# The attention loop of a two-layer encoder, with all its matmuls in 64 rows of the array

## The chip, the cores and the metric

The kernel runs as one program on one core of a Trainium2 chip. The metric is the device time of one execution in microseconds (us). The core has a matrix engine (PE) with its weight load (PEld), three engines for elementwise work (DVE, ACT, POOL), a queue that issues DMAs (SP; POOL and ACT issue some too), an on-chip memory of 128 partitions (SBUF), and an accumulator memory (PSUM) of eight banks of 128 x 512 fp32, into which PE writes and from which DVE and ACT read.

## The reference, cut to what matters

Two layers over two sequences (2048 and 512 tokens, width 1024), each with an RMS norm, a mixer, a SiLU gate, an output projection and a residual. Only the attention layer is touched by the change:

```python
def attention_layer(x, g, w_in, w_out, sink, rel_bias):
    h = rmsnorm(x, g)
    z = h @ w_in                  # q: 16 heads of 64, k and v: 4 heads of 64, gate: 1024
    ...
    # 128-query blocks, each against three 128-key blocks
    scores = einsum('bnqhgd,bnkhd->bnhgqk', qb, kw) * scale + bias
    p = exp(scores - m); denom = p.sum() + exp(sink - m)
    o = einsum('bnhgqk,bnkhd->bnqhgd', p / denom, vw)
    return x + (o * silu(gate)) @ w_out
```

Products are made to near-fp32 precision from two parts of each operand: every logical product of two tiles is three matmuls, high by high, high by low and low by high.

## The kernel before, in words

**Chunks.** The 2560 tokens go through the attention layer in five chunks of 512: chunk 0 is the short sequence, chunks 1 to 4 the long one. Each chunk makes its normalised input (`make_h`), projects k and v (`kv_proj`, L353), and then runs the attention loop (L909) over n = 0 to 16. The output projection of a chunk (`out_proj`, L653) begins inside the loop and ends after it. The Fourier layer follows all chunks.

**One turn of the loop.** A turn works on two query blocks of a head pair p: scores, softmax, transposes, product with v. It is software-pipelined by one turn: in turn n the scores are made of "new" blocks (head pair n // 2, blocks 0, 1 or 2, 3), while the "old" blocks of turn n - 1 are transposed and multiplied by v. Between these, PE works off "fill": the q and gate projections of later head pairs, eight units a turn (a unit is a product of one contraction block k with its three matmuls of 128 x 512; L966 and L980), and near the end the output projection.

**Steps, with their lines.** `scores` (L524; matmuls L530) multiplies q by the key window; the contraction is 64 long, so the two heads of a pair stand in the two halves of the array's rows and run as pairs of 64-row matmuls. `biased` (L545, DVE L549) adds the bias and finds the row maximum, `exps` (ACT L557) takes the exponential, `divide` (DVE reciprocal L565, DVE L569 or ACT L567) normalises. `transp` (L575; PE L589) transposes 64 x 64 pieces, in 64 rows too. `parts` (ACT L597, DVE L598) copies them out of PSUM as a high and a low part. `av` (L600; PE L615) multiplies by v with all 128 rows. `out_evac` copies half of the result to SBUF (ACT L624, tile `t`), adds the other half to it (DVE L633, twice), and POOL, ACT and POOL apply the gate and split the result into tile `uT` (L635, L638, L639). A finished projection is evacuated by `evac_q` (ACT L465, DVE L466) or `evac_g` (ACT L473, DVE L475); in chunk 0 the helper `scaled` first scales it by the norm (DVE L350).

**PSUM.** Each bank is a tile of its own: four turn over in the pool `psum` through `bank` (L76) for projections, transposes, `av` and the output projection, and four (`spt`, L332) hold the scores, one of them also a transpose.

**What sets the order.** `seq` and `pe` (L164, L170) chain the instructions of PE, ACT and DVE inside the loop, each behind the one before it, so each engine runs them in the order in which the code is written. Waits between engines are put in when the program is built: an instruction waits until the counter of another engine has reached the value that the last conflicting access to the same tile sets. In this program they are kept by tile.

## Time and profile before

| | us |
|---|---|
| runs, median of 3 (lowest to highest) | 1570.89 (1569.17 to 1573.85) |
| profiled execution: span from first to last instruction | 1566.4 |
| what lies around the span, median less span | 4.5 |

The page gives no other time of the profiled execution than its span. In the trace the loops of the chunks begin (first matmul of the first q projection) at 30.5, 241.8, 451.1, 664.2 and 871.4 us of the span, and the last `av` of each ends at 184.1, 399.0, 612.1, 825.2 and 1027.5 us; the Fourier layer takes the last third. The page's first part is busy time by engine, the second the span in 40 slices, the fourth the chain of work that ended last, followed back from the last instruction. A row of that chain gives the start of a piece and how long the chain ran in it, so for back-to-back matmuls it gives the time that they took one after the other, whereas a row of the timeline gives the time from the first start to the last end, in which overlapping instructions are merged.

### The profile page before, as it was taken

The page shows a single profiled execution, that of the slowest core. Times are in us where ns is not written, and L with a number is a line of the kernel's source. Part 1 is how long each engine was busy: PE and PEld are TensorE (multiplying, and loading weights), DVE is VectorE, ACT ScalarE, POOL GpSimd, SP SyncE. Part 2 cuts the span into 40 slices and gives each one's busy share as a digit, 9 for nine tenths or more (in the row PEclk, how much of TensorE's full clock was granted, in tenths as well). Part 3 has the DMA queues.
Part 4 walks back from the last instruction along what each step waited for, and adds up shares of the span by engine and source line. Part 5 has one row for each costly group of instructions (what it writes and reads, how often), then busy time and mean ns, then how long its engine had stood idle before and what let it go on. Part 6 is the DMA issues. An engine that isn't in the chain of part 4 may idle for free.

```text
span 1566.4 us, 27701 instructions
## 1 busy us (share of the span) xinstructions
PE 1555.5 (99%) x9818; PEld 1306.6 (83%) x9818; DVE 1178.3 (75%) x2843; ACT 877.1 (56%) x2120; POOL 446.7 (29%) x614
## 2 busy tenths in 40 slices
PE   9999999999999999999999999999999999999998
PEld 7888888888898888988888888888888888888886
DVE  5888555887548886378873588767999888989886
ACT  7788534676237774256761476636556564333353
POOL 2575642421403413124224142123121211101100
PEclk9999999999999999999999999999999999999999
DMA  8588696665865576756749665675675569656852
GB/s 295 203 330 297 222 369 208 214 242 202 294 228 196 207 267 231 245 190 234 267 150 322 239 235 196 227 258 203 217 249 189 195 243 399 210 202 250 296 193 95
DMA packets 100423, 372.34 MB, mean 238 GB/s; under 512 B 11204, under 2 KB 22220, under 8 KB 82877
## 3 DMA queue, kind: packets, MB, share of 16 engines
q1 hardware_dynamic: 82716, 297.38, 54.2%
q0 software_dynamic: 16400, 70.04, 11.5%
q10 hardware_dynamic: 1168, 3.15, 0.6%
q8 instruction: 78, 1.28, 0.3%
q14 instruction: 61, 0.49, 0.1%
HBM read 280.06 MB, written 90.47 MB: 237 GB/s over the span
## 4 chain that ended last, share of the span: by engine, by line
PE 92%; DVE 3%; issue 2%; DMA 1%; POOL 0%; ACT 0%; SPq 0%; POOLq 0%; DVEq 0%; ACTq 0%
PE gp L117 15%; PE qp L117 14%; PE spt L117 11%; PE op L117 7%; PE av L615 6%; PE spt L530 6%; PE W L117 5%; PE fo L117 5%; PE vp L117 3%; PE Wo L117 3%; PE Z L117 3%; PE pt L589 3%; PE Zo L117 2%; PE z L1166 2%; PE ABp L117 1%
## 5 line engine op out<-in xcount | busy, mean ns | idle before, releaser
L117 PE MATMUL gp<-h,wg 128*128 128x512 f32 x960 | 237.8, 396 | 0.0
L117 PE MATMUL qp<-h,wq 128*128 128x512 f32 x960 | 237.1, 396 | 0.0
L549 DVE CUSTOM_DVE_ANT_0 S<-spt,b 128x385 f32<-128x385 f32 (+1 forms) x320 | 161.0, 529 | 98.9 <-PE spt L530 62.4
L117 PEld LDWEIGHTS gp<-h,wg 128*128 128x128 f32 x960 | 174.9, 188 | 37.3 <-issue 1.0
L117 PEld LDWEIGHTS qp<-h,wq 128*128 128x128 f32 x960 | 174.9, 188 | 36.5 <-issue 0.3
L557 ACT ACTIVATE S<-S 128x385 f32<-128x385 f32 (+1 forms) x320 | 190.7, 610 | 15.7 <-DVE S L549 15.7
L597 ACT CAST pts<-pt 128x384 fp32r<-128x384 f32 (+1 forms) x240 | 95.1, 462 | 179.3 <-PE pt L589 176.5
L598 DVE TENSOR_TENSOR pts<-pt,pts 128x384 fp32r<-128x384 f32 (+1 forms) x240 | 112.5, 519 | 22.4 <-ACT pts L597 22.2
L639 POOL TENSOR_TENSOR uT<-o,uT 128x256 fp32r<-128x256 f32 x75 | 55.5, 740 | 234.2 <-ACT uT L638 234.1
L117 PE MATMUL spt<-wo,uT 128*128 128x512 f32 x480 | 120.3, 391 | 0.0
L117 PE MATMUL op<-wo,uT 128*128 128x512 f32 x480 | 118.9, 391 | 0.0
L615 PEld LDWEIGHTS av<-pts,v 128*128 128x128 f32 x576 | 101.4, 188 | 18.8
L615 PE MATMUL av<-pts,v 128*128 128x512 f32 (+1 forms) x576 | 115.7, 341 | 0.0
L117 PE MATMUL fo<-wo,tTu 128*128 128x512 f32 x480 | 115.0, 392 | 0.0
L569 DVE TENSOR_SCALAR S<-S 128x384 f32<-128x384 f32 (+1 forms) x192 | 103.2, 537 | 6.8
L117 PEld LDWEIGHTS op<-wo,uT 128*128 128x128 f32 x480 | 89.4, 188 | 18.5
L117 PEld LDWEIGHTS spt<-wo,uT 128*128 128x128 f32 x480 | 89.1, 188 | 18.3
L530 PE MATMUL spt<-kwin,qab 64*128 64x384 f32 (+1 forms) x960 | 104.1, 343 | 0.0
L117 PEld LDWEIGHTS fo<-wo,tTu 128*128 128x128 f32 x480 | 88.3, 188 | 17.3
L530 PEld LDWEIGHTS spt<-kwin,qab 64*128 64x128 f32 x960 | 75.5, 184 | 28.2 <-issue 25.0
L635 POOL TENSOR_TENSOR o<-o,s 128x256 f32<-128x256 f32 x75 | 55.1, 735 | 129.4 <-DVE o L633 128.6
L589 PEld LDWEIGHTS pt<-ident,S 64*128 64x128 f32 x1328 | 69.8, 138 | 4.4 <-issue 1.8
(342 smaller groups left out, 3207.3 us busy)
## 6 DMA issues: line engine op xcount, KB each, us to landing
wo<-wsd SPq DMA_DIRECT2D x32, 1024.0 KB, 6.5
wq<-wsd SPq DMA_DIRECT2D x31, 1024.0 KB, 7.7
wg<-wsd SPq DMA_DIRECT2D x31, 1024.0 KB, 6.3
x<-x1d SPq DMA_DIRECT2D x40, 512.0 KB, 3.5
b<-b21d SPq DMA_DIRECT2D x40, 512.0 KB, 4.6
b<-rowd SPq DMA_DIRECT2D x40, 384.0 KB, 4.4
xs<-in_x_dram SPq DMA_DIRECT2D x23, 512.0 KB, 6.6
s2d<-gt POOLq DMA_DIRECT2D x40, 256.0 KB, 4.3
```

The lines of the kernel that those rows point to most:

```text
L117: ins = pe(PE.matmul(out, a[i], b[j], start=start and i + j == 0, stop=stop and i == 1, skip_group_check=more))
L530: pe(PE.matmul(banks[j][:, 2 + k0 * P : 2 + k1 * P], res["q"][rows, qp, b * P : (b + 1) * P], kwin[g][rows, kp, b * P + k0 * P : b * P + k ...
L549: seq(DVE, DVE.tensor_tensor_reduce(out=s[:, e0:e1], in0=ps[:, 1 + e0 : 1 + e1], in1=st["bias"][:, j, 386 - e1 : 386 - e0][:, ::-1], scale ...
L557: last_exp[0] = seq(ACT, ACT.activation(s[:, e0:e1], s[:, e0:e1], AF.Exp, bias=s[:, 386:387], scale=-1.0, accum_out=s[:, 387:388]))
L569: seq(DVE, DVE.tensor_scalar(s[:, ks], s[:, ks], den, None, ALU.mult))
L589: pe(PE.transpose(ps[h][:, kb, j, :], ss[j][rows, 1 + kb * P : 1 + (kb + 1) * P], ident[rows, rows]))
L597: seq(ACT, ACT.copy(hi, ps[:, k0:k1]))
L598: seq(DVE, DVE.tensor_tensor(lo, ps[:, k0:k1], f32(hi), ALU.subtract))
L615: pe(PE.matmul(to, v, pt, start=n == part == 0, stop=part == 1 and n in (1, len(todo) - 1), skip_group_check=n > 1,))
L635: eng.tensor_tensor(o, o, s, ALU.mult)
L639: low = eng.tensor_tensor(lo, o, f32(hi), ALU.subtract)
L1166: PE.matmul(to, m[part][:, g * P : (g + 1) * P], ch[:, 0, :, odd * P : (odd + 1) * P], start=part == 0, stop=part == 1,)
```

## The change

All matmuls of the loop now use 64 rows. A product of 128 rows is split into its upper and lower 64 rows; an upper half of one product runs beside a lower half of another, each into its own bank (`beside`). Since the halves of one product meet in one bank, a PE `nop` waits for the last matmul of the one half before the other half begins there (`swapped`). Projections and output tiles go through a new class `Product`, in the order `fills(n)` lists: in turn n the first twelve pairs finish the lower rows of projection n + 1 beside the first upper rows of projection n + 2, the second twelve finish the upper rows of n + 2 beside the first lower rows of n + 3. `av` is split by query block: block 0 in the upper rows beside block 1 in the lower, then the other way round, with three pairs of fill between them. A block's product takes six matmuls of 256 columns in each half, where before two blocks shared matmuls of 512 columns.

The eight banks are now two tiles of four banks each, `pj` (projections and `av`) and `spt` (banks 0, 1 scores, banks 2, 3 transposes), so there are two banks of scores and two of transposes where there were four and three. The turn is written in another order: transpose of the first old block, scores of the first new block, twelve pairs of fill, transpose of the second, scores of the second, nine pairs, first half of `av`, three pairs, second half. `out_evac` of a turn is moved into the next turn, ahead of the copies of `parts`; the evacuation of a projection stands between the softmax of the first and the copies of the second block. Weights are loaded one projection at a time, a little over two turns ahead. The norm's transposes (`spread_halves`) use 64 rows. In `kv_proj` the products go to `spt` and `pj`; the Fourier layer's pool `psum2` is opened after the old pools are closed.

```diff
-    banks = [pstack.enter_context(tc.tile_pool(name="psum", bufs=4, space=PSUM))]
+    banks = []
+    pj = pstack.enter_context(tc.tile_pool(name="psum", bufs=1, space=PSUM)).tile([P, 4, 512], F32, name="pj")
+    spt = pstack.enter_context(tc.tile_pool(name="spsum", bufs=1, space=PSUM)).tile([P, 4, 512], F32, name="spt")
...
+            def beside(*pairs):
+
+                swapped([(unit[0].last, h) for pair in pairs for h, unit in enumerate(pair) if unit is not None])
+                for upper, lower in pairs:
+                    both = []
+                    for h, unit in enumerate((upper, lower)):
+                        if unit is not None:
+                            both.append((unit[0], h) + unit[0].parts(unit[1], slice(64 * h, 64 * h + 64)))
+                    for i, j in ((0, 0), (0, 1), (1, 0)):
+                        for out, h, a, b in both:
+                            out.last[h] = pe(PE.matmul(out.ps, a[i], b[j], **out.flags()))
+
+            def swapped(places):
...
+                if before:
+                    wait = pe(PE.nop())
+                    for ins in before:
+                        tc.add_manual_dep(wait.ins, ins.ins.name, DONE, reason="other rows of a bank")
...
-                    ps = [bank(f"pt{c}_{p}_{b}_{h}")[:, :384] for h in range(2 - second)]
-                    if second:
-                        ps.append(spt[0][:, 2:386])
-                    ps = st["pt", b] = [t.rearrange("p (k j q) -> p k j q", k=3, j=2) for t in ps]
+                    ps = [spt[:, 2 + h, :384].rearrange("p (k j q) -> p k j q", k=3, j=2) for h in range(2)]
...
+                def fills(n):
+
+                    t0, t1, t2, t3 = op_tiles
+                    if n < 14:
+                        x, y, z = (o + (t3,))[n + 1 : n + 4]
+                        return [((y, k), (x, 4 + k)) for k in four], [((y, 4 + k), (z, k)) for k in four]
...
                     if new:
                         one, two = order
                         on_act = new[1] if c else one
-                        new[0].scores(one, spt[:2])
...
+                        new[0].scores(one)
+                    split = out_evac() if out_evac else None
+                    if old:
+                        old[0].parts(older[0])
...
+                    beside(*first)
...
+                    if n < 15:
+                        evacs[n + 1]()
+                        loads[n + 5]()
                     if old:
                         old[0].transp(older[1], 1)
...
+                    cut = 2 if n == 14 else 3
+                    beside(*second[:cut])
                     if old:
...
+                        if n > 14:
+                            places = Both(spt[:, 0:2])
+                        elif n % 4 == 3:
+                            places = [pj[:, 3], pj[:, 0]]
+                        else:
+                            places = Both(pj[:, n % 4 : n % 4 + 2])
+                        halves = old[0].av(old[1], places)
+                        halves[0]()
+                    beside(*second[cut : cut + 1])
```

How the order moves is shown for turn 5 of chunk 2, where the old blocks are blocks 0 and 1 of head pair 2 and projection 6 (q of pair 3) is finished. First PE before, from the last transpose (out to `spt`) over the second half of q's fill (`qp`) to `av` and the gate's fill (`gp`):

```order
L589 MATMUL spt_233<-ident,S_2_1_1_6090 128x64
L117 MATMUL qp_3_6141<-h_4_5121,wq_3_5905 128x512 x3
L117 MATMUL qp_3_6141<-h_5_5130,wq_3_5905 128x512 x3
L117 MATMUL qp_3_6141<-h_6_5138,wq_3_5905 128x512 x3
L117 MATMUL qp_3_6141<-h_7_5146,wq_3_5905 128x512 x3
L615 MATMUL av_2_0_6243<-pts_2_0_6174,v_4_3036 128x512 [waits DVE_49,Activation_49]
L615 MATMUL av_2_0_6243<-pts_2_0_6174,v_4_3036 128x512 [waits DVE_49]
L615 MATMUL av_2_0_6243<-pts_2_0_6174,v_5_5500 128x512 x2
L615 MATMUL av_2_0_6243<-pts_2_0_6174,v_3_3008 128x256 x2
L615 MATMUL av_2_0_6243<-pts_2_0_6174,v_6_5503 128x256 x2
L117 MATMUL gp_3_6269<-h_0_5088,wg_3_5907 128x512 [waits DMAHW5_49,PE_49]
```

The fill between the transposes and `av` waits for no other engine; `av` waits for the transposed parts. PE in the changed kernel, from the end of the `av` before, over the first transpose and the first scores to the first fill:

```order
L658 MATMUL pj<-pts_1_2_7378,v_7_6703 128x256
L623 MATMUL spt<-ident,S_2_0_0_7410 128x64 [waits DVE_49]
L623 MATMUL spt<-ident,S_2_0_0_7410 128x64 x5
L623 MATMUL spt<-ident,S_2_0_1_7412 128x64 x6
L570 MATMUL spt<-kwin,qab_2_7282 128x384 x6
L480 MATMUL pj<-h_0_6274,wg_3_7129 128x512 [waits DVE_49,PE_49,Activation_49]
L480 MATMUL pj<-h_4_6307,wq_3_6963 128x512
L480 MATMUL pj<-h_0_6274,wg_3_7129 128x512
```

The first fill now waits for DVE, ACT and PE: the value of DVE's counter is the one that the second add of `out_evac` (L684 in the changed kernel, on the `av` just ended) sets, ACT's is that of its copy (L675), and PE's is the `nop`'s. The fill writes banks 2 and 3 of `pj` here, the adds read banks 0 and 1. Further on in the same turn, from the end of the first fill to the second:

```order
L480 MATMUL pj<-h_7_6332,wq_3_6963 128x512
L623 MATMUL spt<-ident,S_2_1_0_7475 128x64 [waits DVE_49]
L623 MATMUL spt<-ident,S_2_1_0_7475 128x64 x5
L623 MATMUL spt<-ident,S_2_1_1_7477 128x64 x6
L570 MATMUL spt<-kwin,qab_2_7282 128x384 x6
L480 MATMUL pj<-h_4_6307,wg_3_7129 128x512 [waits DVE_49]
L480 MATMUL pj<-h_0_6274,wq_4_7285 128x512 [waits DMAHW6_49]
L480 MATMUL pj<-h_4_6307,wg_3_7129 128x512
```

The second fill waits for the value that DVE's last instruction of `evac_q` (L516) sets on the projection that the first fill has just finished; it writes banks 3 and 0, the evacuation reads bank 2. The transpose waits for the second `biased` of the new block, which reads banks 0 and 1 of `spt`, where the transpose writes banks 2 and 3. Last, ACT in the changed kernel, from the copy of `out_evac` to the copies of the second old block, with q's evacuation as the eighth row:

```order
L675 COPY t_1_2_7561<-pj 64x512 [waits PE_49]
L632 CAST pts_2_0_7542<-spt 128x6x64 [waits PE_49,Activation_49]
L632 CAST pts_2_0_7542<-spt 128x6x64 [waits DVE_49]
L594 ACTIVATE S_2_2_0_7571<-S_2_2_0_7571 128x385 [waits DVE_49]
L594 ACTIVATE S_2_2_1_7573<-S_2_2_1_7573 128x385 [waits DVE_49]
L689 CAST uT_1_6786<-o_1_2_7563 128x256 [waits Pool_49]
L604 ACTIVATE S_2_2_1_7573<-S_2_2_1_7573 128x384 [waits DVE_49]
L515 ACTIVATE qab_3_7608<-pj 128x512 [waits PE_49]
L632 CAST pts_2_0_7542<-spt 128x6x64 [waits PE_49]
L632 CAST pts_2_0_7542<-spt 128x6x64 [waits DVE_49]
```

Before, q's evacuation stood behind all four copies and all four exponentials of a turn and ahead of `out_evac`; now it stands behind the first block's exponentials and ahead of the second block's copies, and `out_evac` opens the turn.

## The prediction

> **What bounds the kernel now.** I read the page's first two parts, then the chain of waits by engine and line, then the chain in order of time over single turns.

> ```profile
> span 1566.4 us, 27701 instructions
> PE 1555.5 (99%) x9818; PEld 1306.6 (83%) x9818; DVE 1178.3 (75%) x2843; ACT 877.1 (56%) x2120; POOL 446.7 (29%) x614
> PEclk9999999999999999999999999999999999999999
> PE 92%; DVE 3%; issue 2%; DMA 1%; POOL 0%; ACT 0%; SPq 0%; POOLq 0%; DVEq 0%; ACTq 0%
> ```

> PE is busy throughout, at the full granted clock, and 92% of the chain is PE's. So before, DVE (75%) and ACT (56%) have room, and their work costs nothing as long as it lands under matmuls. One turn of chunk 3 in the chain (start, duration):

> ```profile
> 743.21 1.25 PE spt L530 x12
> 744.46 0.43 PE pt L589 x13
> ...
> 745.26 2.95 PE gp L117 x12
> 748.21 1.38 PE av L615 x8
> 749.59 2.75 PE qp L117 x12
> 752.34 0.71 PE spt L530 x5
> ```

> The turn takes 752.34 - 743.21 = 9.13 us and holds no wait: scores 1.25, transposes 0.80 (between 744.46 and 745.26, the rows in between are more of the same), gate fill 2.95, `av` 1.38, q fill 2.75. Twelve matmuls cost 2.75, 0.229 each; 2.95 stands after the 64-row transposes, so going into 128 rows costs 0.20.

> **The change part by part.** *Switches.* A turn goes into 128 rows once (0.20) and back once; scores that open the turn take 1.25, those that follow other 64-row work 1.14 (chunk 1's row below has 1.08), so the way back is 0.11. All in 64 rows saves 0.31 a turn, 75 turns: 23 us. That is the gain.

> *The pairs.* A pair of 64-row matmuls of 512 columns is not in this trace. From below: scores in pairs of 384 columns take 1.14/6 = 0.19; the columns that a 128-row fill streams would take 0.229 x 384/512 = 0.172, so at worst the overhead of 0.018 stays and a pair of 512 is about 0.241 (the line through the 64-column transposes, 0.063 a pair, and 0.19); at best 0.203 (part of the 0.229 being the exposed load). I take 0.229, as the streamed columns are the same, and keep -0.026 x 24 x 75 = -47 and +0.012 x 24 x 75 = +22 for the range. The row of loads that bears on it:

> ```profile
> L117 PEld LDWEIGHTS gp<-h,wg 128*128 128x128 f32 x960 | 174.9, 188 | 37.3 <-issue 1.0
> L530 PEld LDWEIGHTS spt<-kwin,qab 64*128 64x128 f32 x960 | 75.5, 184 | 28.2 <-issue 25.0
> ```

> A 128-row load of 0.188 passes beside matmuls spaced 0.229. [...]

> *New waits.* This is the large term. The order of PE shows that in the changed program the first fill of a turn waits for DVE's second add and ACT's copy of the `av` just ended, and the second fill waits for DVE's evacuation of the projection that the first fill finishes. Neither reads the bank that is written; `pj` is one tile and conflicts are kept by tile. Also the transposes wait for both `biased` of a block that reads the other banks of `spt`. Before, each bank was a tile and these waits were not there. So PE stands, and all of its queue behind it: the weight loads, transposes, scores, hence ACT and DVE too. The durations, from chunk 3:

> ```profile
> 744.87 1.25 ACT L597 CAST pts<-pt 128x384 fp32r<-128x384 f32 x3 [3.02 <-PE pt L589]
> 745.98 0.51 ACT L597 CAST pts<-spt 128x384 fp32r<-128x384 f32 x1
> 746.36 0.65 ACT L557 ACTIVATE S<-S 128x385 f32<-128x385 f32 x1
> 746.87 0.22 ACT L557 ACTIVATION_READ_ACCUMULATOR S<-S 128x1 f32 x1
> 746.97 0.64 ACT L557 ACTIVATE S<-S 128x385 f32<-128x385 f32 x1
> 747.57 0.42 ACT L638 CAST uT<-o 128x256 fp32r<-128x256 f32 x1
> 747.86 0.64 ACT L557 ACTIVATE S<-S 128x385 f32<-128x385 f32 x1
> ...
> 749.12 0.62 ACT L567 ACTIVATE S<-S 128x384 f32<-128x384 f32 x1
> 749.65 0.58 ACT L473 ACTIVATE th<-gp 128x512 f32<-128x512 f32 x1
> 750.25 0.58 ACT L624 COPY t<-av 64x512 f32<-64x512 f32 x1
> ```
> ```profile
> 745.17 0.56 DVE L549 CUSTOM_DVE_ANT_0 S<-spt,b 128x385 f32<-128x385 f32 x1
> 745.65 1.48 DVE L598 TENSOR_TENSOR pts<-pt,pts 128x384 fp32r<-128x384 f32 x3
> ...
> 748.18 0.84 DVE L569 TENSOR_SCALAR S<-S 128x384 f32<-128x384 f32 x1
> 748.94 0.21 DVE L565 RECIPROCAL S<-S 128x1 f32<-128x1 f32 x2
> 749.18 0.42 DVE L569 TENSOR_SCALAR S<-S 128x384 f32<-128x384 f32 x1
> ...
> 750.33 0.69 DVE L475 SCALAR_TENSOR_TENSOR s<-th,gp 128x512 f32<-128x512 f32 x1 [0.19 <-ACT th L473]
> ```
> ```profile
> L633 DVE TENSOR_TENSOR o<-av,t 64x256 f32<-64x256 f32 x150 | 62.5, 416 | 8.2 <-ACT t L624 5.7 <-ACT b L510 1.5
> 665.18 0.26 ACT L370 CAST kwin<-spt 64x128 fp32r<-64x128 f32 x1 [0.54 <-DVE kwin L371]
> 665.48 0.28 DVE L371 TENSOR_TENSOR kwin<-spt,kwin 64x128 fp32r<-64x128 f32 x1 [0.33 <-ACT kwin L370]
> ```

> The last two rows give the hand-over between engines: 665.18 + 0.26 to 665.48, 0.04. Now a turn of the changed kernel by hand, with 0 at the end of the last `av` matmul:

> - PE: transposes of one block 0.80/2 = 0.40, scores 0.57 (half of 1.14), done at 0.97.
> - ACT's copy 0.04 to 0.62; DVE's adds from 0.72 (0.10, as between th's end at 750.23 and 750.33) and 1.15, done at 1.57. With a hand-over and 0.20 to get PE going again (estimate: the price of the switch, 0 to 0.4) the first fill starts at 1.81, not 0.97. **First stall 0.84.** It ends at 1.81 + 2.75 = 4.56.
> - ACT: copies of the transposes 1.01 and 1.38; DVE: their low parts 1.58 and 2.04, `biased` 2.51 and 2.99 (done 3.07, 3.55); ACT: exponentials 3.11 and 3.72 with the accumulator's read to 4.45, `uT` within. DVE: reciprocal and normalising 3.88 to 4.49, second reciprocal by 4.65; ACT's normalising 4.69 to 5.21.
> - Evacuation: behind that in ACT's order, 5.22 to 5.80; DVE's part 5.84 to 6.53. Transposes and scores of the second block pass under it (4.56 to 5.53). Second fill at 6.53 + 0.04 + 0.20 = 6.77, not 5.53. **Second stall 1.24.** Without the evacuation waiting behind the softmax it could start 0.6 earlier; ACT's order forbids it.
> - Nine pairs 2.06, half of `av` 0.69, three pairs 0.69, half of `av` 0.69: end at 10.90. The low parts of the second block are done near 7.5, so `av` waits for nothing.

> So a turn takes 10.90 against 9.13: +1.77, which is 0.84 + 1.24 less 0.31. (PE alone: 8.82.) The other chunks' turns:

> ```profile
> 897.39 2.99 PE gp L117 x12
> ...
> 904.26 1.08 PE spt L530 x12
> ...
> 915.11 2.95 PE gp L117 x12
> ```
> ```profile
> 142.70 2.97 PE gp L117 x12
> ...
> 151.30 2.94 PE qp L117 x12
> ```

> Chunks 1 and 4 take (915.11 - 897.39)/2 = 8.86 a turn, chunk 0 takes 151.30 - 142.70 = 8.60. They have the same chain on ACT and DVE and shorter scores, so after 10.77 and, with chunk 0's extra scaling in each evacuation on DVE, 11.0. Sum: 30 x 1.77 = 53, 30 x 1.91 = 57, 15 x 2.4 = 36, together **146**.

> *On top.* DVE's normalising takes 0.84 instead of 0.42 in about a third of the turns (the row at 748.18 beside that at 749.18): 26 x 0.34 = 9. Turn 15 evacuates nothing: 5 x -1.24 = -6. At a loop's head one `nop`-ordered wait for the first `evac_q` (0.58 + 0.69 + hand-overs and restart, 1.59): 5 x 1.59 = 8; the first and last turn lack one of the waits' cover, 10 x 0.9 = 9. Before the loop:

> ```profile
> 664.19 3.20 PE qp L117 x14
> ...
> 667.50 2.30 PE qp L117 x10
> ...
> 669.38 0.26 ACT L370 CAST kwin<-spt 64x128 fp32r<-64x128 f32 x1 [0.36 <-DVE kwin L371]
> ```

> Before, q's first fill (3.20 + 2.30) ran under the evacuation of k from 664.2 to 669.9; now it writes the tile that this evacuation reads, and waits: 5.7 x 3 = 17 in the chunks with a halo, 2 in chunk 0. In the turns 3, 7 and 11 `av` stands in two places, with two copies and four adds: 15 x 0.35 = 5. The `nop`s wait for matmuls 0.69 or more back (the three pairs between the halves of `av`), so I cost them at nothing; where that cover fails it is about 0.2 each, two a turn, 30. Weights come two turns ahead, 20 us against the 8 us that the page shows from issue to landing: nothing.

> Sum: 146 + 9 - 6 + 8 + 9 + 17 + 2 + 5 = **+190**. The profiled span of 1566.4 plus the 4.5 around it is the median of 1570.9, so 1570.9 + 190 is **1760**.

> **The rivals.** *A: the evacuation is not held up by the softmax.* If ACT gets to it as soon as the first fill ends, that is 4.60 to 5.18, DVE to 5.91, the second fill at 6.15: the stall is 0.62, and 70 x 0.62 = 43 fall off: 1718. For it speaks that ACT is at 56%; against it the written order, in which both exponentials and the normalising stand ahead. Chance 0.12.

> *B, the other side: the waits don't bind.* Everything hangs on two moments: the adds done 0.97 after `av`'s end, and the evacuation done 0.97 after the first fill's end. Then only the switches count: 1570.9 - 23 = 1548. The rows say 1.57 and 1.97; copy and two adds alone are 0.58 + 2 x 0.42 = 1.42, so it would take shorter instructions than the rows have, or pairs that hide more. Chance 0.06.

> *C: the pairs don't run side by side as far as the loads go.* Two loads of 0.184 per pair make 0.37 against 0.229, 0.14 x 24 = 3.4 a turn, of which some 0.6 fits into stalls: 2.8 x 75 = 208 on top, 1969. For it: two loads per pair now stand where one stood. Against it: scores do two loads a pair at 0.19 a pair. Chance 0.05.

> *D: the stalls take the clock down.* PE stands 0.84 and 1.24 in every turn; at half the clock its 8.82 would be 17.6 a turn: 75 x (17.6 - 8.8) = 660 on top, near 2400. In the trace of before the PEclk row stays at 9 and PE has no such gaps to learn from. Chance 0.02. [...]

> *E:* no change at all 0.01 (gain and stalls would have to cancel), slower in some way that I don't see 0.02.

> **How the numbers follow.** The forecast, slower by about 190, has 0.72. 0.3% of the time, 5 us, is what can be told from no change here. Faster: B, 0.06. Same: 0.01. Slower: 0.72 + 0.12 + 0.05 + 0.02 + 0.02 = 0.93. The range: below, A's 1718 with half of the pairs' -47, about 1695; above, 1760 with the pairs' +22, the `nop`s' 30, or the restart's 0.2 more per stall (30), not all at once: 1810. It leaves out B, C, D and E and the tails.

> **What would show it.** In the changed profile PE's busy share falls from 99% and ACT and DVE enter the chain; ahead of the first fill's matmuls PE stands some 0.8 with DVE's add as releaser, ahead of the second some 1.2 with the evacuation's DVE instruction; a turn of chunk 3 takes 10.9; twelve pairs take 2.75; the chain's rows no longer have a 2.95 beside a 2.75. Stalls under 0.3, a turn under 9, or 24 pairs far from 5.5 would make the prediction wrong; so would a wait of the transposes for `biased`, which I found to be over in time.

## The result, and the profile after

The changed kernel takes 1901.28 us (median of 4 runs, 1895.81 to 1909.83) against 1570.5 for the kernel before: ratio 1.211, 95% interval 1.207 to 1.215. The prediction was 1760, with a range up to 1810. The direction is right; of the 331 us lost the prediction had 190.

The page of the changed kernel, first its span, busy times, granted clock and the shares of the chain:

```profile
span 1904.0 us, 34005 instructions
PE 1627.0 (85%) x13123; PEld 1382.5 (73%) x13123; DVE 1201.1 (63%) x2853; ACT 912.3 (48%) x2135; POOL 444.5 (23%) x614
PEclk9889989999899999998999999999999999999999
PE 47%; DVE 19%; ACT 17%; issue 5%; DMA 3%; POOL 1%; SPq 0%; DVEq 0%; POOLq 0%; ACTq 0%
```

PE fell from 99% to 85% of the span and from 92% to 47% of the chain; DVE and ACT, which together had 3% of it, have 36%. None of the two became much busier (DVE 1178 to 1201 us, ACT 877 to 912), so no engine's capacity is the bound. They are on the chain because the others wait for them. And the clock row, all 9 before, now has 8s (mean granted clock 1.000 before, 0.970 now).

What PE waits for (engine, tile and line, releaser; us in total, times, longest):

```profile
PE pj L480 <- DVE o L684: 89.9, 62, 6.7
PE pj L480 <- DVE s L525: 56.3, 40, 3.3
PE pj L480 <- DVE qab L516: 47.3, 35, 2.5
PE pj L445 <- DVE kwin L379: 10.1, 3, 3.8
```

The first is the stall that the prediction called the first (fill behind the adds of `out_evac`, 1.45 a time), the next two are the second (fill behind the evacuation of a projection, 103.6/75 = 1.38 a time). In the regular turn below they are 0.78 and 1.53; twelve long ones, of 2.0 to 6.7 us, raise the mean of the first. Both are there, at the predicted places, with the predicted releasers. The chain in order of time over a regular turn of chunk 3, whose transposes begin at 971.68 and those of the next turn at 983.39, that is 11.71 us:

```profile
971.13 0.73 PE pj L658 x12
...
971.88 0.59 ACT t L675
...
972.57 0.42 DVE o L684
...
973.00 0.42 DVE o L684
...
973.45 0.57 DVE pts L633
...
974.04 0.49 ACT pts L632
...
974.55 0.56 DVE pts L633
975.11 0.48 DVE S L586 x2
...
975.62 1.31 ACT S L594 x4
976.92 0.30 ACT uT L689
977.22 0.56 ACT S L604
977.78 0.49 ACT th L523
...
978.36 0.69 DVE s L525
```

Behind the first row, the second half of the `av` before, no piece of it is PE's: ACT and DVE hand work to each other for the whole turn. The place where this turn departs from the one that the prediction worked out is at 973.45 to 974.55, where DVE subtracts, then ACT copies, then DVE subtracts. The prediction had ACT's two copies back to back. In the timeline (the bracket is idle time ahead and its releaser):

```profile
972.88 0.48 ACT L632 CAST pts<-spt 128x384 fp32r<-128x384 f32 x1 [0.42 <-PE spt L570]
974.04 0.48 ACT L632 CAST pts<-spt 128x384 fp32r<-128x384 f32 x1 [0.68 <-DVE pts L633]
979.10 0.49 PE L480 MATMUL pj<-h,wq 64*128 64x512 f32 x1 [1.53 <-DVE s L525]
```

ACT's second copy reads bank 3 of `spt`, DVE's first subtraction reads bank 2, and yet the copy waits for it. Here two engines that only read one PSUM tile are put in order as well, and ACT stood 0.68 us for it. (Both also write the tile `pts`; run 3 below leaves that as it is, and there the two subtractions run back to back, 1.02 us for both.) The row for it stood in the ACT order shown with the change (the second copy waits for DVE); its price was overlooked.

### The profile page after: what moved, and what is told of

It is laid out like the page before. It is cut to its first block, busy times and chain, and to the rows that moved or that the text cites. A ratio compares the mean times of both kernels' runs of the same rounds, so it can differ in the third digit from the quotient of the medians.

```text
span 1904.0 us, 34005 instructions
## 1 busy us (share of the span) xinstructions
PE 1627.0 (85%) x13123; PEld 1382.5 (73%) x13123; DVE 1201.1 (63%) x2853; ACT 912.3 (48%) x2135; POOL 444.5 (23%) x614
## 4 chain that ended last, share of the span: by engine, by line
PE 47%; DVE 19%; ACT 17%; issue 5%; DMA 3%; POOL 1%; SPq 0%; DVEq 0%; POOLq 0%; ACTq 0%
PE pj L480 11%; PE pj L120 6%; PE spt L120 6%; DVE pts L633 5%; ACT S L594 5%; PE W L120 4%; PE pj L658 3%; ACT pts L632 3%; DVE o L684 3%; PE fo L120 3%; PE Wo L120 3%; DVE S L586 2%; PE Z L120 2%; ACT t L675 2%; ACT S L604 2%
## 5 line engine op out<-in xcount | busy, mean ns | idle before, releaser
L480 PE MATMUL pj<-h,wg 64*128 64x512 f32 x1800 | 482.5, 410 | 78.8 <-DVE qab L516 47.3
L480 PE MATMUL pj<-h,wq 64*128 64x512 f32 x1680 | 445.8, 407 | 95.3 <-DVE s L525 50.9
L480 PEld LDWEIGHTS pj<-h,wg 64*128 64x128 f32 x1800 | 330.5, 192 | 118.3 <-DVE qab L516 58.5
L480 PEld LDWEIGHTS pj<-h,wq 64*128 64x128 f32 x1680 | 305.9, 191 | 133.3 <-DVE s L525 62.1
L633 DVE TENSOR_TENSOR pts<-spt,pts 128x384 fp32r<-128x384 f32 (+1 forms) x320 | 169.5, 530 | 115.8 <-ACT pts L632 113.4
L632 ACT CAST pts<-spt 128x384 fp32r<-128x384 f32 (+1 forms) x320 | 146.1, 456 | 184.1 <-DVE pts L633 140.0
L480 PE MATMUL pj<-wo,uT 64*128 64x512 f32 x660 | 116.9, 430 | 22.3 <-DVE o L684 16.9
L684 DVE TENSOR_TENSOR o<-pj,t 64x256 f32<-64x256 f32 (+1 forms) x170 | 62.9, 370 | 111.3 <-ACT t L675 100.2
L658 PEld LDWEIGHTS pj<-pts,v 64*128 64x128 f32 x1568 | 123.7, 189 | 11.8 <-DVE pts L633 0.9
L658 PE MATMUL pj<-pts,v 64*128 64x256 f32 x1568 | 126.7, 282 | 0.3 <-DVE pts L633 0.2
L623 PE MATMUL spt<-ident,S 64*128 64x64 f32 x1792 | 85.9, 224 | 19.0 <-DVE pts L633 11.7
```

Of the source, the lines that this page charges most:

```text
L480: out.last[h] = pe(PE.matmul(out.ps, a[i], b[j], **out.flags()))
L623: pe(PE.transpose(ps[h][:, kb, j, :], ss[j][rows, 1 + kb * P : 1 + (kb + 1) * P], ident[rows, rows]))
L632: seq(ACT, ACT.copy(hi, ps[:, k0:k1]))
L633: seq(DVE, DVE.tensor_tensor(lo, ps[:, k0:k1], f32(hi), ALU.subtract))
L658: last[i][h] = pe(PE.matmul(places[i][:, :256], v[rows], pt[rows], start=not swap and n == 0, stop=swap and n == len(todo[h]) - 1, skip_gr ...
L684: seq(DVE, DVE.tensor_tensor(o[64 * j : 64 * j + 64, at], ps[0:64, :, j], t2[:, at, j], ALU.add))
```

## The experiments

To state expectations I used a schedule made of rows, a calculation and so an estimate: every engine takes its instructions in the written order, each with the mean duration of its row in the profile of the changed kernel or the one before, and each waits for what the built program makes it wait for. It knows nothing of the granted clock. For the kernel before it gives 1560 (span 1566.4), for the changed kernel 1853 (1904.0). Theory W below is that PE, ACT and DVE wait for accesses to other banks of the same four-bank tile.

**1. One tile for each bank.** `Banks` holds four tiles of 128 x 512 and is indexed as the large tile was.

```diff
-    pj = ....tile([P, 4, 512], F32, name="pj")
-    spt = ....tile([P, 4, 512], F32, name="spt")
+    pj = Banks(..., "pj")
+    spt = Banks(..., "spt")
...
-                            places = Both(pj[:, n % 4 : n % 4 + 2])
+                            places = [pj[:, n % 4], pj[:, (n + 1) % 4]]
```

> The changed kernel with each of the eight PSUM banks a tile of its own (order of the work, pairs and nops unchanged; av always writes two one-bank tiles, so its evacuation is two copies and four adds a turn instead of one and two). Theory W (PE stands for work on other banks of the same four-bank tile): the waits of the fill for the adds and the evacuation vanish, and so does the second copy of the transposed parts waiting for DVE's subtraction on the other bank; a schedule of each engine's instructions in the written order with the durations of the changed kernel's rows gives 178 us less than the same schedule of the changed kernel, a turn of chunk 3 of 9.8 to 10.3 instead of 11.7, and most of the 56 us at a lowered clock go too: 1690, between 1660 and 1725. Theory P (the 64-row pairs are dear in themselves, by their loads or the clock): all pairs are still there, so it stays above 1860.

1706.88, ratio 1.0871 (1.0852 to 1.0889). Pairs, `nop`s and order are the same (two copies and four adds now evacuate each `av`, which is more work, and the last sum of a chunk goes to SBUF instead of PSUM), so 194 of the 331 us hang on how eight banks are grouped into tiles. What PE still waits for:

```profile
PE spt L632 <- DVE pts L642: 33.1, 29, 8.4
PE pj L667 <- DVE pts L642: 25.2, 60, 0.6
PE pj L667 <- ACT pts L641: 8.8, 9, 2.9
```

The fill is all but gone from the list (0.7 us, once). `av` (L667 here) waits for the parts of the second block, a wait that the data demand.

**2 and 3. Only one of the two tiles taken apart**, `pj` in run 2, `spt` in run 3:

```diff
-    pj = ....tile([P, 4, 512], F32, name="pj")
+    pj = Banks(..., "pj")
```
```diff
-    spt = ....tile([P, 4, 512], F32, name="spt")
+    spt = Banks(..., "spt")
```

> Only the four banks of projections and av are tiles of their own; scores and transposes still share one tile. Theory W: fill no longer waits for adds or evacuation, but the transposes of the second block come to wait for the second biased of the first block (the stall moves there, about 1.3 us in each turn), and av for the parts: a turn of 11.0 to 11.5 in chunk 3, 63 us saved and some of the lowered clock: 1820, between 1790 and 1850. If the stall at the fill is all that matters, this run equals the one with all banks apart, 1690.

> Only the four banks of scores and transposes are tiles of their own; projections and av still share one tile. Theory W: the stalls of the fill stay, but the chain on ACT and DVE is shorter, since copies and subtractions of the transposed parts no longer take turns: 10.9 a turn in chunk 3 instead of 11.7, which is the turn that the prediction had, 75 us saved: 1820, between 1795 and 1850. If the taking of turns is covered elsewhere, it stays at 1900.

1816.9 (ratio 1.1587, 1.1568 to 1.1607) and 1825.18 (1.1624, 1.1605 to 1.1644). Each alone gives 84 and 76 us, both together 194: each alone leaves the other tile's stalls, which take up a part of what it gains. With `pj` apart the stall moves to the transposes, as expected:

```profile
PE spt L632 <- DVE S L595: 84.4, 68, 6.1
PE pj L667 <- ACT pts L641: 40.9, 53, 1.6
```

With `spt` apart the turn-taking is gone and most turns of chunk 3 are 10.95 to 11.1 us (those whose `av` stands in two places 11.46) where the prediction's turn, made without turn-taking, was 10.90.

**4. Copies written ahead of the subtractions.**

```diff
                     for h in range(2):
...
                         seq(ACT, ACT.copy(hi, ps[:, k0:k1]))
-                        seq(DVE, DVE.tensor_tensor(lo, ps[:, k0:k1], f32(hi), ALU.subtract))
+                        todo.append((lo, ps[:, k0:k1], f32(hi)))
+                    for lo, ps, hi in todo:
+                        seq(DVE, DVE.tensor_tensor(lo, ps, hi, ALU.subtract))
```

> The changed kernel with one edit: in parts, both of ACT's copies are written ahead of DVE's two subtractions, so that the second copy does not wait for the first subtraction; tiles as in the changed kernel. Theory W: the chain of ACT and DVE gets shorter in both blocks of a turn, partly given back since the first subtraction now waits for the second copy: 36 us less, 1865, between 1835 and 1880. If this taking of turns costs nothing: 1901.

1864.25 (1.1886, 1.1867 to 1.1906). Writing both copies ahead of both subtractions, with nothing else changed, brings 37 us. So here the order of reads of one tile by two engines is kept, and it costs these 37 us.

**5 and 9. Another order for ACT and DVE, on separate tiles.** The steps of a turn, as they were written and as they are now (`one` and `two` are the new blocks, `split` is the last part of `out_evac`):

```diff
-out_evac  parts(0)  biased(one)  exps(one)  split  divide(one)  evac  parts(1)  biased(two)  exps(two)  divide(two)
+parts(0)  biased(one)  out_evac  exps(one)  evac  parts(1)  divide(one)  split  biased(two)  exps(two)  divide(two)
```

> The kernel with a tile for each bank, and the turn written in another order for ACT and DVE: copies of the transposed parts of the first block, biased, copy and adds of the av before, exponentials, evacuation of the projection, parts of the second block, and only then the normalising of the first. PE's order, its pairs and the nops are unchanged. Theory W with chain C (what is left of the loss in the run with separate tiles, 138 us, is a turn of ACT and DVE one after the other, 9.9 to 10.4 us in chunk 3, in which av waits for the parts that stand behind the evacuation): the schedule of the rows gives 52 us less than for that run: 1655, between 1635 and 1680; a turn of chunk 3 of 8.8 to 9.4. If the 138 us are PE's own (nops, loads, pairs): no change, 1707.

1637.57 (1.0447, 1.0428 to 1.0465). In this run, and in 6 and 8, the fill of turn 15 writes a bank before `out_evac` has read it, so the attention output of blocks 2 and 3 of head pair 6 is lost in each chunk; the amount of work is the same. Run 9 writes `out_evac` first in that turn and computes everything:

> The reordered kernel with one tile for each bank once more, with one difference: in turn 15 the copy and adds of the av before are written ahead of the first fill, which there writes a bank that they read (in the earlier reordered runs that fill came first and the av of one turn a chunk was lost). Both theories: one turn of 17 a chunk changes its order, so the time stays that of the reordered kernel within 5 us: 1637.

1634.2 (1.0423, 1.0405 to 1.044). So of the 138 us left by run 1 another 73 were the order in which ACT and DVE take their work. PE is back at 97% of the span:

```profile
span 1630.8 us, 34482 instructions
PE 1575.7 (97%) x13123; PEld 1384.7 (85%) x13123; DVE 1188.0 (73%) x2983; ACT 896.1 (55%) x2200; POOL 445.6 (27%) x614
```

It is the fastest form with the loop in 64 rows here, and still 4% slower than the kernel before. From the first to the last scores chunk 0 takes 156.0 (before 125.9), the chunks 1 to 4 take 135.2, 141.4, 140.6 and 136.4 (131.5, 134.9, 134.9, 130.7): about half of what is left is chunk 0.

**6. The fill back in 128 rows, on separate tiles and with the new order.**

```diff
-                    beside(*first)
+                    if wide:                  # turns 0 to 11
+                        for k in four:
+                            o[n + 1].whole(4 + k)
+                    else:
+                        beside(*first)
...
-                    beside(*second[:cut])
+                    if wide:
+                        for k in four:
+                            o[n + 2].whole(k)
+                    else:
+                        beside(*second[:cut])
```

> The reordered kernel with one tile for each bank, but the projections' fill of turns 0 to 11 in 128 rows again (four contraction blocks of projection n + 1 as first fill, four of n + 2 as second, all four ahead of av); scores, transposes and av stay in 64 rows. So two blocks of 128-row work a turn, two switches there and back, and no fill between the halves of av. If pairs cost what 128-row matmuls do and a switch there and back 0.31, as the prediction had it, 60 turns x 2 x 0.31 = 37 us more, less what PE had to wait in them anyway: 1680, between 1665 and 1700 (or 25 over the run beside it). If 64-row pairs are dear (loads): faster than the reordered kernel.

1670.85 (1.0652, 1.0634 to 1.067), 33 us over run 5, which loses the same values. The chain over one turn of chunk 3 is PE's alone:

```profile
994.18 0.52 PE spt L632 x12
994.70 0.58 PE spt L579 x6
995.28 2.94 PE pj L129 x12
998.23 0.93 PE pj L667 x12
```

A fill costs 2.94 instead of 2.75, and the half of `av` behind it 0.93 instead of the 0.73 of the changed kernel, where 64-row work stands ahead of it. The run makes 120 switches there and back that run 5 does not make, so one costs some 0.28 (33/120) where the prediction had 0.31. The gain that the change is built on is real and has about the size that the prediction gave it.

**7. The kernel before, with its scores in one tile.**

```diff
-            spt = []
-            for i in range(4):
-                spt.append(spsum.tile([P, 512], F32, name=f"spt{i}"))
+            spt4 = spsum.tile([P, 4, 512], F32, name="spt4")
+            spt = [spt4[:, i] for i in range(4)]
```

> The kernel before with one edit: its four banks of scores are one tile of four banks; everything else, all 128-row matmuls too, is as before. Theory W: waits come by the tile whatever the rows of the matmuls, so the fourth transpose and the second scores come to wait for biased on other banks, and in the projections of k and v the copies and subtractions take turns: the schedule of the rows gives 117 us more than for the kernel before: 1695, between 1660 and 1730. If tiles of several banks cost nothing: 1570.

1691.33 (1.0773, 1.0755 to 1.0791). No matmul has changed its rows, no instruction its place; four banks became one tile, and it costs 122 us. The waits that PE got:

```profile
PE spt L588 <- DVE S L548: 43.8, 60, 1.2
PE spt L117 <- DVE pts L597: 16.9, 10, 2.2
```

**8. The new order on the changed kernel's two tiles.**

> The changed kernel, its two tiles of four banks each kept, with the same new order of ACT and DVE as the reordered kernel. Theory W: the fill waits for the evacuation and now the second scores wait for parts and biased as well, so that the order alone brings nothing: the schedule of the rows gives 27 us more than for the changed kernel: 1925, between 1890 and 1950. If the written order of ACT and DVE is the cause and the tiles only add to it: about 52 us less, 1850.

1966.87 (1.2527, 1.2506 to 1.2548): slower than the changed kernel, and beyond the upper end expected. That the order alone brings nothing is confirmed. The excess goes with the clock, which cost 121 us of full-speed time against 56 in the changed kernel (table below): PE stands twice in quick succession here. Two turns of chunk 3 are cut below into windows of 3.41 us, at the edges at which the clock of this trace changes (window, its length, then busy time of PE, PEld, DVE, ACT, POOL with counts, granted clock, DMA share, GB/s):

```profile
997.90:1001.31 3.41, 2.26 (x30) 1.96 (x28) 2.04 (x7) 1.90 (x5) 0.00 (x0) 1.00 0.26 50
1001.31:1004.72 3.41, 2.00 (x20) 1.42 (x18) 2.09 (x5) 1.86 (x5) 0.72 (x1) 1.00 0.63 264
...
1011.55:1014.96 3.41, 0.91 (x10) 0.48 (x6) 3.10 (x8) 2.65 (x7) 2.00 (x3) 1.00 0.80 250
1014.96:1018.38 3.42, 3.13 (x14) 2.47 (x16) 2.77 (x10) 1.40 (x4) 0.00 (x0) 0.50 0.23 91
```

The stalls in them (PE's timeline, idle time in brackets):

```profile
1000.91 0.79 PE L570 MATMUL spt<-kwin,qab 64*128 64x384 f32 x6 [1.15 <-DVE S L586]
...
1003.12 0.50 PE L480 MATMUL pj<-h,wg 64*128 64x512 f32 x1 [1.41 <-DVE qab L516]
...
1012.81 0.80 PE L570 MATMUL spt<-kwin,qab 64*128 64x384 f32 x6 [1.14 <-DVE S L586]
...
1015.25 0.79 PE L480 MATMUL pj<-h,wq 64*128 64x512 f32 x1 [1.65 <-DVE s L525]
```

From 1011.55 to 1014.96 PE was busy for 0.91 us; then the clock is 0.50 for the whole next window, and the first fill matmul takes 0.79 instead of the 0.50 of the turn before. The two stalls of that turn fall into different windows, on either side of 1001.31, and each leaves PE busy for 2.00 or more.

**10. No later weights in chunk 0's loop.**

```diff
-LATE = (8, 9)
-AGAIN = (0, 10, 11, 12)
+LATE = ()
+AGAIN = (0, 8, 9, 10, 11, 12)
```

> The changed kernel without the two loads of later chunks' weights that stand inside chunk 0's loop (after turns 2 and 4); those two weights are read again in chunk 1 instead, as four others are. Theory L (in chunk 0 ACT stands in front of a weight's copy until POOL and a store have freed its buffer, and since the changed PE waits for ACT, PE stands with it): the two gaps of PE of 5.45 and 5.07 us in chunk 0 shrink to the ordinary 1.5, and the halved clock behind them goes: the chunk's first to last scores take 180 to 188 instead of 198, of which chunk 1's head gives back about 5: 1890, between 1878 and 1898. If chunk 0's loss is the same chain as in the other chunks and the scaling on DVE: its loop stays at 198 and the time at 1901 or above.

1897.87 (1.2104, 1.207 to 1.2138), not to be told from the changed kernel. The two gaps did go, and chunk 0's loop went from 198.0 to 191.1 us, less than theory L had; chunk 1's head gave back 6.4 (103.6 to 110.0 between the loops). The time at a lowered clock did not shrink: by windows of 10 us, either trace went without 15.4 us of full-speed time in its first 250 us. Other places of chunk 0 were at a lowered clock instead, such as 90 to 100 and 120 to 130 us (0.83 each, 1.00 in the changed kernel). So the waits of ACT for a weight's buffer are a small part, some 7 us, of the 72 that chunk 0 lost.

## Why the prediction fell short

**What held.** The mechanism: both stalls, their releasers and the sign. The pairs: 24 matmuls of 512 columns in 64 rows take what twelve of 128 rows took (first fill 973.56 to 976.40, 2.84 with its restart, against 2.75 and 0.20 for the switch before), so rival C falls. The switches: run 6. Rival A falls, since the evacuation does wait behind the softmax, and rival B, since the waits bind.

**The step that failed first: the line "ACT: copies of the transposes 1.01 and 1.38".** Counted from the start of the transposes at 971.68, the first fill begins at 1.88 (predicted 1.81), but the second copy at 2.36, the second fill at 7.42 (6.77) and the turn ends at 11.71 (10.90). Of the 0.81, 0.65 is there at the second fill, and the idle time of the second copy is 0.68: copies and subtractions taking turns. The other 0.16 lies in PE's own stretch behind it (4.29 us from the second fill to the end, worked out as 4.13). 0.65 x 75 is 49 us of the missing 141, and the 0.16 another 12. Run 3, in which each bank of `spt` is a tile, has the predicted turn (10.95 to 11.1) and is 76 us faster: 52 of them between the first and last scores of the loops, though only 1 of these in chunk 0, and most of the rest between the loops, where copies and subtractions of k and v take turns too. Run 4 shows the turn-taking by itself.

**The step that failed second: "before the loop", 17 + 2 + 8 us.** Outside the span from first to last scores of the five loops the changed profile loses 13.5 us ahead of the first loop, 66 between loops (20.8, 16.7, 19.5, 9.2) and 10.6 behind the last, 90 in all. The prediction counted one evacuation in each chunk with a halo. In the changed kernel matmuls cover little of the evacuations of k and v, since the next ones write the same tile, and copies and subtractions take turns too. Chunk 1's head in the chain:

```profile
329.46 0.70 DVE kwin L379
330.19 0.59 ACT kwin L378
...
330.80 0.70 DVE kwin L379
...
331.55 3.15 PE pj L120 x24
...
340.96 0.30 DVE kwin L379
...
341.31 7.76 PE pj L120 x24
```

Two gaps of 2.5 us stand between the rows at 331.55 and 341.31, and 24 matmuls of 128 rows, 5.5 us by the 0.229 of the prediction, then take 7.76, the first 4.30 of them at a granted clock of 0.50 (338.78 to 345.61). With `pj` apart (run 2) the four stretches between loops shrink from 103.6, 94.6, 97.6 and 81.4 to 91.8, 84.5, 85.3 and 81.1; with all banks apart to 85.9, 79.2, 80.9 and 78.2 (before: 82.8, 77.9, 78.1 and 72.2).

**The step that failed third: rival D, the clock, at 0.02 and all or nothing.** The 0.02 was an estimate: the trace of before, at a granted clock of 1.000, shows nothing to work it out from. The rival came true in part. The two stalls of the regular turn, 0.78 and 1.53, stand 4 us apart, and the granted clock is 1.00 from 972 to 984 us (in the page's row most slices of the loops are 9, some 8). Behind some longer ones it fell to 0.50. At the end of chunk 1's loop PE stands for 3.31 us, from 514.38 (PE's timeline, then windows as above, again cut where the clock changes):

```profile
517.70 0.76 PE L480 MATMUL pj<-wo,uT 64*128 64x512 f32 x1 [3.31 <-DVE o L684]
```

```profile
509.44:512.85 3.41, 3.41 (x36) 2.95 (x37) 2.53 (x9) 1.88 (x6) 0.00 (x0) 1.00 0.56 238
512.85:516.27 3.42, 1.53 (x31) 1.33 (x27) 0.48 (x2) 0.45 (x2) 0.00 (x0) 1.00 0.47 120
516.27:519.68 3.41, 1.98 (x10) 1.75 (x12) 2.39 (x7) 1.35 (x4) 0.73 (x1) 0.50 0.00 0
519.68:523.10 3.42, 3.42 (x22) 2.78 (x20) 0.87 (x5) 1.77 (x6) 0.74 (x1) 0.50 0.00 0
523.10:526.51 3.41, 2.90 (x35) 2.19 (x31) 2.04 (x5) 1.56 (x3) 0.00 (x0) 1.00 0.58 195
```

The add that releases PE there is only the last link. Ahead of the copy that feeds it, ACT stands for a DMA, the bias of the last head pair:

```profile
515.80 0.20 ACT L550 COPY b<-sk 128x4 f32<-128x4 f32 x1 [3.00 <-DMA b<-rowd]
```

The same wait stands at the end of the loops of chunks 0, 2 and 3 (5.88, 2.76 and 2.59 us), and the stalls of PE behind the four are 6.68, 3.31, 2.67 and 2.51, 15 us together. In the kernel before, ACT waited there too (0.99 to 1.87), but PE did not wait for ACT. The prediction had a line for the loads of the weights, and none for that of the bias. Why this DMA lands late is not settled.

Summed over a trace up to its last matmul, time x (1 - granted clock) says how much full-speed time a run went without. Beside it stands what the schedule of rows, blind to the clock, falls short of the span:

| kernel | schedule | span | span less schedule | clock lost |
|---|---|---|---|---|
| before | 1560 | 1566.4 | 6 | 0 |
| changed | 1853 | 1904.0 | 51 | 56 |
| 1, a tile for each bank | 1675 | 1706.8 | 32 | 24 |
| 4, copies first | 1817 | 1861.7 | 45 | 48 |
| 5, a tile for each bank, reordered | 1623 | 1635.0 | 12 | 10 |
| 7, before, scores in one tile | 1677 | 1692.2 | 15 | 17 |
| 8, order only | 1880 | 1970.2 | 90 | 121 |

The two columns on the right go together, so some 50 of the changed kernel's 331 us are PE at half speed after its own stalls. This is a reading of the traces with an estimate beside it; no run kept PE busy through a stall to take the clock's part away alone.

**By place.** Between the profiled executions, whose spans differ by 338 us, the loops lose 72.1, 43.5, 46.5, 45.7 and 39.6 us from first to last scores in chunks 0 to 4, 247 together, of which the prediction had 163; outside them 90, of which it had 27. Of the 84 that were missing in the loops the turn-taking is some 50 and the four stalls for the bias are 15; the parts overlap with the clock and are not additive. Chunk 0 was set at 36 or a little more and lost 72: its stalls are longer (ACT and DVE also prepare weights there, and the wait for the bias is its longest) and 12 of the clock's 56 us are lost in it. How its loss divides between these is not settled; run 10 removed one suspect and found it small. In run 9, too, ACT waits 6.60 us for the bias at the end of chunk 0's loop.

## What to carry to other kernels

Before banks are gathered into one tile, ask who will then wait for whom: in this program conflicts on PSUM are kept by tile, and the price was 122 us in a kernel where nothing else changed (run 7); reads of one tile by two engines count among them (37 us in run 4). When a schedule is worked out by hand, price every wait that the order shows, also one between engines that were never late before, and one for a DMA that was hidden before. A stall of PE that was long (3.31 us at the end of chunk 1's loop), or two that followed closely (1.14 and 1.65 in run 8), cost twice here: the granted clock was 0.50 for the matmuls behind it, and the first of the fill took 0.76 and 0.79 instead of 0.50.

## What was not expected of the hardware

So it mattered in these traces where a stall fell. In run 8 the stalls of 1.15 and 1.41 us fell into two windows, busy for 2.26 and 2.00, and the clock stayed at 1.00; of the next turn's, the 1.14 and most of the 1.65 fell into one, busy for 0.91, and the clock behind it was 0.50. Nor was the window ahead of 516.27 an idle one: PE had stood for only 1.9 of its 3.42 us.
